# Two adaLN groups of layer 1 moved beside its modulation, and local attention scores in two passes with stacked parts

## The chip, the cores and the metric

The kernel runs on one core of a Trainium2 chip. A core has TensorE (PE in the profile), VectorE (DVE), ScalarE (ACT), GpSimd (POOL), and SyncE (SP), whose queue issues most of the loads. The metric is the device time of one execution in microseconds; smaller is better.

## The reference

Two layers over 256 context and 256 latent tokens of width 1024. Each modulates its input by adaLN, runs three token mixers (S5, latent attention, local attention), merges them with gates, and then runs sixteen experts of which each takes the tokens it wants. Only the latent stream is returned, so layer 1 updates no context.

```
def adaln_params(cond, lp):
    return jnp.split(jax.nn.silu(cond) @ lp['w_ada'] + lp['b_ada'], 6, axis=-1)
...
def trunk_layer(xc, xl, c, c_ctx, lp, row, col, update_ctx):
    mod_l = [m[:, None, :] for m in adaln_params(c, lp)]
    ...
    hl = modulate(xl, mod_l[0], mod_l[1])
    yc, yl = token_mixer(hc, hl, lp, row, col, update_ctx)
    xl = layer_norm(ALPHA * xl + mod_l[2] * yl, lp['ln1_g'], lp['ln1_b'])
    fl = expert_choice_ffn(modulate(xl, mod_l[3], mod_l[4]), lp)
    xl = layer_norm(ALPHA * xl + mod_l[5] * fl, lp['ln2_g'], lp['ln2_b'])
...
def window_branch(qc, kc, vc, ql, kl, vl, sink, row, col, update_ctx):
    ...
    qb = axial_rope(q, row, col)...          # latent queries, rotated
    s_band = jnp.einsum('bnqkgd,bnskd->bnkgqs', qb, kb) * WIN_SCALE      # banded, rotated keys
    s_ctx = jnp.einsum('bnqkgd,bskd->bnkgqs', qpb, kc) * WIN_SCALE       # plain queries, context keys
    p = jax.nn.softmax(jnp.concatenate([s_band, s_ctx, sk], axis=-1), axis=-1)
```

The six modulation vectors form three groups of two (group 0: the mixer's shift and scale; 1: its gate and the experts' shift; 2: the experts' scale and gate). A layer's input product and S5 need group 0 only.

## The kernel before

An fp32 product whose operands are activations and weights is made of f32r parts: `split` and `put` (L428 to L436) write a high part by ScalarE and the difference by VectorE or GpSimd, and `mm3` adds three products, high by high, high by low, low by high. All matmuls are issued from one line, L247, transposes from L250, loads from L233, so a row is told from another by its tile: `sc`, `mm`, `F`, `ad` and `tp` are PSUM tags, `big` holds the queries and keys of the attentions, `extra` and `wc` the parts of branch outputs and weights, `arena` everything else in fp32.

**adaLN groups.** `ada_group(l, g)` (L377) loads sixteen pieces of `w_ada`, 512 KB each, through a ring of staging buffers, and multiplies each by four fp32 matmuls of 32 columns, side by side in four column groups, into the bank `ad`: 64 matmuls a group, which the profile records twice each. Then come one addition, four transposes and the copies into `modT`. In layer 0 the groups (layer 0; 1), (0; 2), (1; 0), (1; 1), (1; 2) stand in the queue `adaq`. `step()` (L211) runs one piece of filler from `fillq` (gates, branch products) and then as much of `adaq` as the filler's cost times `ADA` allows. The mixers call `tick()` to let filler in between their own rows; the order of each engine is then set by a scheduler from dependencies and its own estimates. Layer 1's groups 1 and 2 end up between the gated unit of S5 (about 264 us) and the end of layer 0's local attention (402 us).

**Layer 1's front.** `modulated_split` (L492) finishes the layer norm of each row block, transposes it (two `tp` banks of four), and writes high and low parts of the modulated rows by ScalarE (L521) and VectorE (L522). `step` of `s5_product` multiplies them by the first columns of `w_in`, four chunks of 128x2x512, into four banks (`mm`, `mm`, `F`, `ad`).

**Local attention.** `win_proj` builds per pair of heads the plain queries QP, the rotated queries QR and the keys KW, each with its high and low part as separate columns, head a on rows 64a to 64a+63. The rotation multiplies by a 128x128 permutation, two f32r passes for queries and one fp32 matmul for keys, and adds cosine and sine products (L1249 to L1251). `win_branch` scores a tile of head a and 128 queries by `mm3` on the head's 64 rows, against 256 context and 256 latent keys: six passes of 256 columns, then a mask of 128 by an identity product. Layer 0 has sixteen such latent tiles and eight context tiles (six passes, no mask), layer 1 sixteen latent tiles. Softmax follows (maximum L1062, exponential L1069, normalisation L1075), then transposes and the product with the values.

Of the kernel before, what the change touches and what calls it, by code (L numbers as in the profile page):

```python
# [45 lines left out]
def _constants():  # L46
# [27 lines left out]

    _ROUND.append(np.concatenate([pm, np.where(k <= q, 0.0, big)], 1).astype(np.float32))
    parts["iota"] = np.tile(np.arange(1, 33, dtype=np.float32), (128, 1))
# [85 lines left out]
class Net:  # L162
# [329 lines left out]
    def modulated_split(self, l, x, in_place, step, stats):  # L492
# [37 lines left out]
        step(part, 3)  # L530
        next(self.first, None)
        self.unrot(htmp=3)
# [697 lines left out]
    def win_proj(self, l, h, full):  # L1230
# [4 lines left out]
        self.bg = [self.block(f"big{i}", F32R) for i in range(3 if full else 2)]  # L1235
        parts = lambda i, o, f, n: self.bg[i][:, o:o + 2 * f * n].rearrange("p (f r n) -> p f r n", f=f, r=2)
        QP, QR, KW = parts(0, 0, 4, NQ), parts(1, 0, 4, 256), parts(1, 2048, 2, 512)
        kf = self.buf("wkf", 512)

        def rope(dst, src, two=None):  # L1240
# [10 lines left out]
            nc.gpsimd.tensor_tensor(dst if two is None else t1, t1, t2, op=OP.add)  # L1251
            if two is not None:
                self.put(dst, t1)
            self.free("wr1", "wr2")
# [7 lines left out]
        v.tensor_copy(kf[:, 0:256], kp[:, 0:256])  # L1262
        rope(kf[:, 256:512], kp[:, 256:512])
        for kv in range(2):
            own, other = [slice(64 * a, 64 * a + 64) for a in (kv, 1 - kv)]
            self.put(KW[own, kv], kf[own])
            self.copy(KW[other, kv], KW[own, kv].bitcast(F32), "a" if kv else "v")
        for f in range(4):
            pt = self.ps("mm" if f % 2 == 0 else "F")
            w = self.wchunk(self.w_in(l, 1184 + f * 128, 1312 + f * 128), KT, 128)  # L1270
            for k in range(KT):
                self.mm3(pt[:, q0:], w(k), h(k, slice(q0, 512)), k == 0, k == KT - 1)
            self.put(QP[:, f], pt[:, q0:])
            rope(QR[:, f], pt[:, 256:], QP[:, f, :, 256 - q0:])
        self.free("wkf", "wkp")
        return QP, QR, KW

    def win_branch(self, l, Z, QP, QR, KW, full, tick):
# [5 lines left out]
        rows = [slice(0, 64), slice(64, 128)]  # L1284
        two = lambda t, c: (t[:, 0, c], t[:, 1, c])
        pv = lambda t: t.rearrange("p (a n) -> p a n", a=2)
        for hp in range(4):
# [3 lines left out]
            for qt in range(2):  # L1291
# [4 lines left out]
                for a in range(2):  # L1296
                    self.mm3(sc[a][:, 0:256], two(QP[rows[a], hp], qc), two(KW[rows[a], kv], slice(0, 256)), True, True)
                for a in range(2):
                    self.mm3(sc[a][:, 256:512], two(QR[rows[a], hp], qs), two(KW[rows[a], kv], slice(256, 512)),
                             True, False)  # L1300
                for a in range(2):
# [6 lines left out]
            if full:  # L1308
                sc = [self.ps("sc").rearrange("p (a n) -> p a n", a=2) for _ in range(2)]
                for qt in range(2):  # L1310
                    for a in range(2):
                        self.mm3(sc[a][:, qt], two(QP[rows[a], hp], slice(qt * 128, qt * 128 + 128)),
                                 two(KW[rows[a], kv], slice(0, 256)), True, True)
                for a in range(2):
# [412 lines left out]
    def build(self, layers=(0, 1), stop=None):  # L1727
# [3 lines left out]
        with tc.tile_pool(name="main", bufs=1) as main, \  # L1731
# [10 lines left out]
            self.const = main.tile([128, NCONST], F32, name="const")  # L1742
            self.round = main.tile([128, 384], F32R, name="round")
            self.idnr, self.permr, self.maskr = [self.round[:, 128 * i:128 * i + 128] for i in range(3)]
            arena = main.tile([128, self.ARENA_COLS], F32, name="arena")
# [49 lines left out]
    def layer(self, l, x, nxt):  # L1795
# [5 lines left out]
        with tc.tile_pool(name=f"parts{l}", bufs=1, reuse_waits="tile") as self.R:  # L1801
# [3 lines left out]
            if full:  # L1805
                self.load(self.const[:, 128:], self.ins["const"][:, 128:])
                self.load(self.buf("round", 256), self.ins["round"])
            h = self.modulated_split(l, x, [full or t < 2 for t in range(4)], step, self.stats)
            self.free(*[f"x{t}" for t in range(4 if full else 2)])
            if full:  # L1810
                nc.scalar.activation(self.round[:, 0:128], self.c("idn"), AF.Copy)
                nc.scalar.activation(self.round[:, 128:], self.A.at("round", 256), AF.Copy)
                self.free("round")
# [134 lines left out]
    ADA = [1.0, 0.4]  # L1948

    FEED_OUT = [[0, 1] * 4, [0, 1] * 4]  # L1950
    FEED_BRANCH = [0, 1]
# [74 lines left out]
```

## Time and profile before

| | |
|---|---|
| median of the runs | 2080.92 us |
| lowest and highest | 2080.52, 2082.33 us |
| profiled execution | 2081.91 us |
| its span | 2080.1 us |
| granted TensorE clock, mean | 0.917 |
| TensorE, VectorE, ScalarE, GpSimd busy | 87%, 50%, 29%, 21% |

The profiled execution took 1.8 us more than its span. The shares are averages over stages with different limits, so stages are to be read one by one. In the span, layer 0's mixer ends near 410 us, its experts fill the time to about 1190 us, layer 1's mixer starts at 1222 us, and its experts end the program.

### The profile page before, as it was taken

How to read it: one execution, taken by the hardware profiler on the slowest of the kernel's cores; microseconds unless marked ns; L12 is line 12 of the kernel's file. 1: busy time of each engine (PE TensorE's matmuls, PEld its weight loads, DVE VectorE, ACT ScalarE, POOL GpSimd, SP SyncE). 2: the span in 40 equal slices, each digit the busy share in tenths (PEclk: the TensorE clock that was granted, in tenths of full speed). 3: DMA queues.
4: the chain of work that ended last, by engine and by line, in shares of the span. 5: the costliest groups of instructions: out<-in, count | busy, mean ns of one | idle time of the engine just before them, and what ended most of it. 6: DMA issues, size and time to landing. Idle time of an engine off the chain costs nothing.

```text
span 2080.1 us, 31699 instructions
## 1 busy us (share of the span) xinstructions
PE 1800.9 (87%) x12421; PEld 1116.5 (54%) x12421; DVE 1030.1 (50%) x2433; ACT 603.5 (29%) x1354; POOL 444.6 (21%) x590
## 2 busy tenths in 40 slices
PE   7898999999998699999799979999998876676665
PEld 5866566677776534334233358887886532232222
DVE  6867656656537712323465276977767321010102
ACT  3354343444433321000111075354553100000000
POOL 4745420011135100001334034640114000000000
PEclk9999999999999899999999989998999887686867
DMA  9256736222237689999999813541367799999996
GB/s 348 80 158 226 245 120 200 92 71 72 63 132 264 262 332 421 421 422 415 417 415 349 335 47 99 155 121 51 103 216 301 282 421 421 421 421 422 420 421 279
DMA packets 173013, 543.88 MB, mean 261 GB/s; under 512 B 18752, under 2 KB 101952, under 8 KB 122688
## 3 DMA queue, kind: packets, MB, share of 16 engines
q1 hardware_dynamic: 172864, 541.86, 68.4%
q8 instruction: 98, 1.61, 0.3%
q14 instruction: 51, 0.42, 0.1%
HBM read 540.77 MB, written 1.05 MB: 260 GB/s over the span
## 4 chain that ended last, share of the span: by engine, by line
PE 55%; DMA 25%; DVE 14%; issue 2%; ACT 2%; POOL 2%; SPq 0%; POOLq 0%; DVEq 0%; ACTq 0%
PE sc L247 17%; PE mm L247 16%; PE F L247 13%; DMA arena<-in_w_down 5%; PE ad L247 4%; PE tp L250 4%; DMA arena<-in_w_up 4%; DMA arena<-in_w_gate 3%; DVE wc L431 2%; DVE arena L572 2%; DMA big<-in_w_gate 2%; DMA h<-in_w_gate 2%; DMA arena<-in_w_in 2%; DMA arena<-in_w_ada 2%; DVE arena L885 1%
## 5 line engine op out<-in xcount | busy, mean ns | idle before, releaser
L247 PE MATMUL F<-h,wc 128*128 128x256 f32 (+1 forms) x1200 | 233.3, 345 | 2.0 <-DVE wc L431 2.0
L247 PE MATMUL sc<-arena,xs 128*32 128x256 f32 (+1 forms) x1336 | 190.4, 528 | 40.1 <-DMA arena<-in_w_up 23.3
L428 ACT ACTIVATE wc<-arena 128x512 fp32r<-128x512 f32 (+2 forms) x280 | 170.6, 619 | 180.6 <-PE F L247 63.7
L250 PE MATMUL tp<-const,arena 128*128 128x128 f32 (+2 forms) x815 | 141.7, 297 | 79.1 <-DVE arena L291 12.2
L247 PEld LDWEIGHTS F<-h,wc 128*128 128x128 f32 x1200 | 185.8, 191 | 33.2 <-issue 6.2
L247 PE MATMUL mm<-arena 128*32 128x256 f32 (+5 forms) x1244 | 186.8, 462 | 17.3 <-DMA arena<-in_w_down 10.0
L431 DVE TENSOR_TENSOR wc<-arena,wc 128x512 fp32r<-128x512 f32 (+2 forms) x205 | 158.9, 787 | 84.6 <-ACT wc L428 84.0
L431 POOL TENSOR_TENSOR wc<-arena,wc 128x512 fp32r<-128x512 f32 (+2 forms) x75 | 98.1, 1307 | 382.6 <-ACT wc L428 340.3
L1678 DVE TENSOR_TENSOR arena<-mm,arena 32x512 f32<-32x512 f32 (+1 forms) x128 | 70.9, 554 | 217.4 <-PE mm L247 215.9
L250 PEld LDWEIGHTS tp<-const,arena 128*128 128x128 f32 (+2 forms) x815 | 97.8, 149 | 145.0 <-issue 35.6
L242 ACT ACTIVATE arena<-tp 128x512 f32<-128x512 f32 (+3 forms) x142 | 62.1, 463 | 346.3 <-PE tp L250 301.9
L247 PEld LDWEIGHTS sc<-arena,xs 128*32 128x32 f32 (+1 forms) x1336 | 61.1, 132 | 144.7 <-issue 76.7
L247 PEld LDWEIGHTS mm<-arena 128*32 128x32 f32 (+2 forms) x1244 | 76.8, 137 | 102.0 <-issue 51.9
L247 PE MATMUL sc<-h,xs 128*32 128x256 f32 (+1 forms) x752 | 110.8, 526 | 19.9 <-DMA h<-in_w_gate 11.2
L264 POOL TENSOR_TENSOR lnq<-lnq,k 128x1 f32<-128x1 f32 x22 | 14.4, 658 | 501.4 <-DVE lnq L311 471.1
L1655 DVE TENSOR_TENSOR arena<-arena,sc 128x512 f32<-128x512 f32 (+1 forms) x32 | 17.8, 555 | 181.3 <-PE sc L247 181.0
L247 PE MATMUL sc<-big,xs 128*32 128x256 f32 (+1 forms) x632 | 86.0, 525 | 23.8 <-DMA big<-in_w_up 12.7
L1653 ACT ACTIVATE arena<-sc 128x512 f32<-128x512 f32 (+1 forms) x32 | 15.7, 491 | 290.9 <-PE sc L247 290.9
L247 PE MATMUL mm<-wc,h 128*128 128x512 f32 (+2 forms) x288 | 81.3, 406 | 6.2 <-DVE wc L431 2.8
L247 PE MATMUL F<-extra,wc 128*128 128x256 f32 (+1 forms) x432 | 83.4, 337 | 3.1 <-DVE smst L1060 2.1
L1654 DVE SCALAR_TENSOR_TENSOR arena<-arena,sc 128x512 f32<-128x512 f32 (+1 forms) x32 | 17.7, 554 | 135.3 <-ACT arena L1653 135.2
L247 PEld LDWEIGHTS sc<-h,xs 128*32 128x32 f32 (+1 forms) x752 | 36.7, 132 | 87.2 <-issue 60.5
(366 smaller groups left out, 3165.4 us busy)
## 6 DMA issues: line engine op xcount, KB each, us to landing
arena<-in_w_up SPq DMA_DIRECT2D x65, 1024.0 KB, 16.6
arena<-in_w_down SPq DMA_DIRECT2D x61, 1024.0 KB, 19.8
arena<-in_w_gate SPq DMA_DIRECT2D x48, 1024.0 KB, 19.5
h<-in_w_gate SPq DMA_DIRECT2D x41, 1024.0 KB, 13.9
arena<-in_w_ada SPq DMA_DIRECT2D x80, 512.0 KB, 5.8
arena<-in_w_in SPq DMA_DIRECT2D x66, 512.0 KB, 3.9
big<-in_w_up SPq DMA_DIRECT2D x26, 1024.0 KB, 19.8
h<-in_w_down SPq DMA_DIRECT2D x26, 1024.0 KB, 18.5
```

The lines of the kernel that those rows point to most:

```text
L242: self.nc.scalar.activation(out, in_, AF.Copy)
L247: return self.nc.tensor.matmul(out, lhsT, rhs, start=start, stop=stop, skip_group_check=True)
L250: self.nc.tensor.transpose(out, in_, self.c("idn")[:n, :n])
L264: self.nc.gpsimd.tensor_tensor(out, in_, e.to_broadcast(list(in_.shape)), op=OP.pow)
L428: nc.scalar.activation(hi, src, AF.Copy)
L431: eng.tensor_tensor(lo, src, hi.bitcast(F32), op=OP.subtract)
L572: tt = lambda o, a, b, op: keep[0](v.tensor_tensor(o, a, b, op=op))
L885: v.tensor_tensor_scan(z, rb, z, 0.0, op0=OP.mult, op1=OP.add)
L1653: nc.scalar.activation(th, gu[0][:, :NF], AF.Tanh, scale=0.5)
L1654: v.scalar_tensor_tensor(th, th, 1.0, gu[0][:, :NF], op0=OP.add, op1=OP.mult)
L1655: v.tensor_tensor(th, th, gu[1][:, :NF], op=OP.mult)
L1678: v.tensor_tensor(YS[n][o:o + 32, c * NF:(c + 1) * NF], yp[r:r + 32, :NF], m5[r:r + 32], op=OP.mult)
```

## The change

Layer 0 no longer queues layer 1's groups 1 and 2. A generator `ada_behind` runs them in layer 1 while `modulated_split` runs: ahead of each pair of transposed units it advances by as many steps as `BEHIND` says, a step being two loads and eight matmuls. It has a ring of ten buffers and uses a bank of tag `sc`; what is left runs behind the last unit.

In the local attention the parts of a head are stacked on the rows: of head a, the rows 64a hold the high part and the other 64 rows the low part, and the keys the other way round. A score is then one pass over the head's 64 rows (high by high) and one over all 128 rows (high by low plus low by high): two passes where there were three. For this `put_heads` writes each half of the rows apart, and the rotation is made by two 64x64 fp32 matmuls.

```
@@ ada
+    def ada_behind(self, l):
+        stg = self.astg
+        self.astg = self.rot("ast", 1024, 10)
+        rows = [self.buf(f"adar{i}", 512) for i in range(2)]
+        gens = [self.ada_group(l, g, True, "sc", rows[g - 1]) for g in (1, 2)]
+        for n in self.BEHIND:
+            for _ in range(n):
+                while gens and next(gens[0], None) is None:
+                    gens.pop(0)
+            yield
+        for g in gens:
+            for _ in g:
+                pass
...
@@ modulated_split
         step(part, 3)
-        next(self.first, None)
+        for _ in self.first:
+            pass
...
@@ win_proj
+        def put_heads(dst, src):
+            for a in range(2):
+                nc.scalar.activation(dst[rows[a], a], src[rows[a]], AF.Copy)
+                v.tensor_tensor(dst[rows[1 - a], a], src[rows[a]], dst[rows[a], a].bitcast(F32), op=OP.subtract)
...
-            if two is None:
-                self.mm(pp[:, :256], self.permr.bitcast(F32), src, True, True)
-            else:
-                for r in range(2):
-                    self.mm(pp[:, :256], self.permr, two[:, r], r == 0, r == 1)
+            for r in rows:
+                self.mm(pp[r, :256], self.permr[r].bitcast(F32), src[r], True, True)
...
-            self.put(QP[:, f], pt[:, q0:])
-            rope(QR[:, f], pt[:, 256:], QP[:, f, :, 256 - q0:])
+            put_heads(QP[:, f], pt[:, q0:])
+            self.copy(kp[:, 0:256], pt[:, 256:], "a")
+            rope(QR[:, f], kp[:, 0:256])
...
@@ win_branch
+        def score(out, q, k, a, qc, kc, stop):
+            self.mm(out, q[rows[a], a, qc], k[rows[a], 1 - a, kc], True, False)
+            self.mm(out, q[:, a, qc], k[:, a, kc], False, stop)
...
-                    self.mm3(sc[a][:, 0:256], two(QP[rows[a], hp], qc), two(KW[rows[a], kv], slice(0, 256)), True, True)
+                    score(sc[a][:, 0:256], QP[:, hp], KW[:, kv], a, qc, slice(0, 256), True)
...
@@ the layer
+            if not full:
+                self.first = self.ada_behind(l)
...
-                self.adaq += [self.ada_group(nxt, g) for g in range(3)]
+                self.adaq += [self.ada_group(nxt, 0)]
...
+    BEHIND = (0, 0, 2, 3, 3, 3, 3, 2)
```

Three places show how the rows move. First TensorE in the second half of layer 0's local attention: `sc` are the scores, `tp` the transposes of probabilities, `mm` their products with the values, `F` the branch products that serve as filler, `ad` group 2 of layer 1. Before:

```order
L247 MATMUL ad_3233<-arena,silu_c 32x256 x8
L250 MATMUL tp_3375<-const,arena 128x128
L247 MATMUL mm_3324<-arena 64x256
L247 MATMUL sc_3326<-big_2418,big_2417 128x256 x6
L250 MATMUL tp_3381<-const,arena 128x128
L250 MATMUL tp_3375<-const,arena 128x128 x3
L250 MATMUL tp_3381<-const,arena 128x128 x3
L247 MATMUL sc_3412<-big_2418,big_2417 128x256 x3
L247 MATMUL sc_3412<-big_2418 128x256 x3
L247 MATMUL sc_3412<-round 128x128
L247 MATMUL ad_3233<-arena,silu_c 32x256 x12
```

The change, where the second half begins:

```order
L247 MATMUL F_3350<-extra_2632,wc 128x512
L247 MATMUL sc_3082<-big_2396,big_2395 128x256 x2
L247 MATMUL sc_3082<-big_2396 128x256 x2
L247 MATMUL sc_3082<-round 128x128
L250 MATMUL tp_3045<-const,arena 128x128 x4
L247 MATMUL mm_2998<-arena 64x256
L247 MATMUL sc_3083<-big_2396,big_2395 128x256 x2
L247 MATMUL sc_3083<-big_2396 128x256
L250 MATMUL tp_3051<-const,arena 128x128 x4
L247 MATMUL sc_3083<-big_2396 128x256
L247 MATMUL sc_3083<-round 128x128
L247 MATMUL mm_2998<-arena 64x256 x4
```

The adaLN rows are gone, and the last row of filler now stands ahead of the first score of the second half; none stands behind it until the attention ends.

Second, TensorE at the front of layer 1: `tp` are the transposes of the modulation, `mm`, `F` and `ad` with `wc` the four banks of the S5 input product. Before:

```order
L250 MATMUL tp_8487<-const,arena 128x128 x3
L250 MATMUL tp_8497<-const,arena 128x128 x3
L250 MATMUL tp_8507<-const,arena 128x128 x4
L250 MATMUL tp_8517<-const,arena 128x128 x4
L250 MATMUL tp_8527<-const,arena 128x128 x4
L247 MATMUL mm_8481<-wc,h_8485 128x512 x2
L247 MATMUL mm_8482<-wc,h_8485 128x512 x2
L247 MATMUL F_8483<-wc,h_8485 128x512 x2
L247 MATMUL ad_8484<-wc,h_8485 128x512 x2
```

The change, with `sc_8300` the bank of group 1:

```order
L250 MATMUL tp_8279<-const,arena 128x128 x3
L250 MATMUL tp_8289<-const,arena 128x128 x3
L247 MATMUL sc_8300<-arena,silu_c 32x256 x16
L250 MATMUL tp_8321<-const,arena 128x128 x4
L247 MATMUL sc_8300<-arena,silu_c 32x256 x20
L250 MATMUL tp_8361<-const,arena 128x128 x4
L247 MATMUL sc_8300<-arena,silu_c 32x256 x8
L250 MATMUL tp_8401<-const,arena 128x128 x4
L247 MATMUL sc_8300<-arena,silu_c 32x256 x8
L247 MATMUL mm_8273<-wc,h_8277 128x512
L247 MATMUL mm_8274<-wc,h_8277 128x512
L247 MATMUL F_8275<-wc,h_8277 128x512
```

Fifty-two matmuls of group 1 (thirteen loads) now stand ahead of the first row of the product; the other seventy-six of groups 1 and 2 (nineteen loads) stand in sixteen pieces between the product's rows that follow.

Third, SP's queue, behind the last loads of layer 0's experts (`in_w_down`). Before:

```order
L233 DMA h_5760<-in_w_down 128x2048 x2
L233 DMA h_5761<-in_w_down 128x2048 x2
L233 DMA arena<-in_w_in 128x2x512 x2
L233 DMA arena<-in_w_in 128x2x288
L233 DMA arena<-in_w_in 128x2x128
L233 DMA arena<-in_w_in 128x2x288
L233 DMA arena<-in_w_in 128x2x128
L233 DMA arena<-in_w_in 128x2x288
L233 DMA arena<-in_w_in 128x2x128
```

The change:

```order
L233 DMA h_5552<-in_w_down 128x2048 x2
L233 DMA h_5553<-in_w_down 128x2048 x2
L233 DMA arena<-in_w_ada 128x1024 x6
L233 DMA arena<-in_b_rep 128x512
L233 DMA arena<-in_w_ada 128x1024 x7
L233 DMA arena<-in_w_in 128x2x512
L233 DMA arena<-in_w_ada 128x1024 x10
L233 DMA arena<-in_w_in 128x2x512
L233 DMA arena<-in_w_ada 128x1024
L233 DMA arena<-in_w_in 128x2x288
L233 DMA arena<-in_w_in 128x2x128
L233 DMA arena<-in_w_ada 128x1024 x2
```

The four chunks of `w_in` for the product stood directly behind the experts' weights; now the first stands behind thirteen loads of `w_ada` and the second behind twenty-three.

## Rows read from the trace of the kernel before

**Rows 1.** The page's busy line: us, share of the span, instructions.

```profile
PE 1800.9 (87%) x12421; PEld 1116.5 (54%) x12421; DVE 1030.1 (50%) x2433; ACT 603.5 (29%) x1354; POOL 444.6 (21%) x590
```

**Rows 2.** Windows of layer 0's mixer: length, engines' busy us (instructions), clock, DMA share, GB/s.

```profile
264.80:310.00 45.20, 45.20 (x216) 27.84 (x215) 26.26 (x57) 21.71 (x47) 13.46 (x16) 1.00 0.37 116
310.00:357.90 47.90, 47.66 (x309) 31.56 (x308) 32.30 (x101) 16.61 (x51) 2.40 (x2) 1.00 0.61 195
357.90:402.40 44.50, 43.32 (x293) 27.87 (x292) 31.14 (x105) 18.21 (x56) 2.58 (x2) 0.95 0.44 141
```

**Rows 3.** Waits of TensorE from 264 to 402 us: total, times, longest.

```profile
PE tp L250 <- DVE arena L1075: 1.2, 1, 1.2
```

**Rows 4.** Windows of the expert stage and of layer 1, columns as above.

```profile
740.00:1190.00 450.00, 424.69 (x2086) 161.34 (x2084) 162.28 (x485) 57.30 (x148) 72.57 (x199) 0.99 0.99 404
1190.00:1202.00 12.00, 10.68 (x28) 4.15 (x24) 9.77 (x22) 4.57 (x12) 2.82 (x5) 1.00 0.00 1
1202.00:1222.20 20.20, 6.14 (x22) 3.61 (x20) 18.52 (x44) 15.27 (x31) 8.54 (x11) 0.62 0.09 27
1222.20:1249.00 26.80, 26.72 (x109) 25.77 (x110) 15.02 (x24) 21.07 (x38) 6.51 (x8) 0.90 0.29 83
1249.00:1284.00 35.00, 35.00 (x250) 31.88 (x250) 17.29 (x29) 22.21 (x46) 12.09 (x15) 1.00 0.33 91
1284.00:1386.00 102.00, 93.51 (x969) 85.09 (x966) 86.60 (x167) 41.30 (x114) 56.98 (x75) 0.97 0.47 135
1386.00:1401.50 15.50, 14.20 (x110) 13.37 (x108) 15.13 (x36) 11.67 (x22) 7.25 (x6) 1.00 0.35 109
1401.50:1428.60 27.10, 27.04 (x194) 23.15 (x195) 23.52 (x78) 13.25 (x36) 5.44 (x5) 1.00 0.31 95
1428.60:1457.50 28.90, 25.24 (x121) 17.22 (x119) 17.51 (x63) 10.71 (x33) 0.00 (x0) 0.70 0.06 18
```

**Rows 5.** Timeline of TensorE between the layers: start, us, what, idle before.

```profile
1219.96 1.08 PE L250 MATMUL tp<-const,arena 128*128 128x128 f32 x4 [2.64 <-DVE arena L522]
```

**Rows 6.** Windows of layer 0's mixer, tile ad alone.

```profile
264.80:357.90 93.10, 16.24 (x168) 5.26 (x168) 0.68 (x1) 0.00 (x0) 1.00 0.49 157
357.90:402.40 44.50, 6.60 (x88) 2.37 (x88) 0.69 (x1) 0.00 (x0) 0.95 0.44 141
```

**Rows 7.** Window of the second half of layer 0's attention, tile F alone.

```profile
357.90:402.40 44.50, 6.81 (x24) 4.28 (x24) 1.38 (x2) 0.00 (x0) 0.95 0.44 141
```

**Rows 8.** Timeline of TensorE in layer 1's local attention.

```profile
1421.08 1.63 PE L247 MATMUL F<-extra,wc 128*128 128x256 f32 x12
...
1428.31 0.45 PE L247 MATMUL F<-extra,wc 128*128 128x256 f32 x2
...
1434.26 0.62 PE L247 MATMUL sc<-big,big 64*128 64x256 f32 x3
...
1435.42 0.62 PE L247 MATMUL sc<-big,big 64*128 64x256 f32 x3
...
1438.73 0.77 PE L247 MATMUL sc<-big,big 64*128 64x256 f32 x3 [1.84 <-ACT arena L1069]
```

**Rows 9.** Timeline of TensorE in layer 0, with adaLN products of group 2.

```profile
384.70 1.50 PE L247 MATMUL ad<-arena,silu_c 128*32 128x256 f32 x24
386.13 1.08 PE L247 MATMUL mm<-arena 128*64 128x256 f32 x8
...
388.89 0.64 PE L247 MATMUL ad<-arena,silu_c 128*32 128x256 f32 x8
389.46 0.62 PE L247 MATMUL sc<-big,big 64*128 64x256 f32 x3
```

**Rows 10.** Timeline of VectorE where layer 1's local parts are built.

```profile
1394.21 1.40 DVE L436 TENSOR_TENSOR big<-arena,big 64x512 fp32r<-64x512 f32 x2
1395.64 0.42 DVE L436 TENSOR_TENSOR big<-F,big 128x256 fp32r<-128x256 f32 x1
```

**Rows 11.** Timeline of ScalarE in the same stretch.

```profile
1394.29 0.39 ACT L435 ACTIVATE big<-F 128x256 fp32r<-128x256 f32 x1
```

More of the change, by code (lines that the diff above doesn't have):

```diff
@@ L73, in _constants @@
     big = np.float32(-1e30 / WIN_SCALE)
-    _ROUND.append(np.concatenate([pm, np.where(k <= q, 0.0, big)], 1).astype(np.float32))
+    _ROUND.append(np.concatenate([pm[:, 0:64] + pm[:, 64:128], np.where(k <= q, 0.0, big)], 1).astype(np.float32))
     parts["iota"] = np.tile(np.arange(1, 33, dtype=np.float32), (128, 1))
@@ L1237, in win_proj, with rope @@
         QP, QR, KW = parts(0, 0, 4, NQ), parts(1, 0, 4, 256), parts(1, 2048, 2, 512)
+        rows = [slice(0, 64), slice(64, 128)]
+        def put_heads(dst, src):
+            for a in range(2):
+                nc.scalar.activation(dst[rows[a], a], src[rows[a]], AF.Copy)
+                v.tensor_tensor(dst[rows[1 - a], a], src[rows[a]], dst[rows[a], a].bitcast(F32), op=OP.subtract)
         kf = self.buf("wkf", 512)
-        def rope(dst, src, two=None):
+        def rope(dst, src, two=True):
             pp = self.ps("sc")
-            if two is None:
-                self.mm(pp[:, :256], self.permr.bitcast(F32), src, True, True)
-            else:
-                for r in range(2):
-                    self.mm(pp[:, :256], self.permr, two[:, r], r == 0, r == 1)
+            for r in rows:
+                self.mm(pp[r, :256], self.permr[r].bitcast(F32), src[r], True, True)
             t1 = self.buf("wr1", 256)
@@ L1250, in rope @@
             v.tensor_tensor(t2, pp[:, :256], self.c("wsin"), op=OP.mult)
-            nc.gpsimd.tensor_tensor(dst if two is None else t1, t1, t2, op=OP.add)
-            if two is not None:
-                self.put(dst, t1)
+            nc.gpsimd.tensor_tensor(t1 if two else dst, t1, t2, op=OP.add)
+            if two:
+                put_heads(dst, t1)
             self.free("wr1", "wr2")
@@ L1262, in win_proj @@
         v.tensor_copy(kf[:, 0:256], kp[:, 0:256])
-        rope(kf[:, 256:512], kp[:, 256:512])
+        rope(kf[:, 256:512], kp[:, 256:512], False)
         for kv in range(2):
             own, other = [slice(64 * a, 64 * a + 64) for a in (kv, 1 - kv)]
-            self.put(KW[own, kv], kf[own])
-            self.copy(KW[other, kv], KW[own, kv].bitcast(F32), "a" if kv else "v")
+            hi, lo = KW[own, kv, 1 - kv], KW[own, kv, kv]
+            nc.scalar.activation(hi, kf[own], AF.Copy)
+            v.tensor_tensor(lo, kf[own], hi.bitcast(F32), op=OP.subtract)
+            self.copy(KW[other, kv], KW[own, kv, ::-1].bitcast(F32), "a" if kv else "v")
         for f in range(4):
@@ L1296, in win_branch @@
                 for a in range(2):
-                    self.mm3(sc[a][:, 0:256], two(QP[rows[a], hp], qc), two(KW[rows[a], kv], slice(0, 256)), True, True)
+                    score(sc[a][:, 0:256], QP[:, hp], KW[:, kv], a, qc, slice(0, 256), True)
                 for a in range(2):
-                    self.mm3(sc[a][:, 256:512], two(QR[rows[a], hp], qs), two(KW[rows[a], kv], slice(256, 512)),
-                             True, False)
+                    score(sc[a][:, 256:512], QR[:, hp], KW[:, kv], a, qs, slice(256, 512), False)
                 for a in range(2):
@@ L1311, in win_branch @@
                     for a in range(2):
-                        self.mm3(sc[a][:, qt], two(QP[rows[a], hp], slice(qt * 128, qt * 128 + 128)),
-                                 two(KW[rows[a], kv], slice(0, 256)), True, True)
+                        score(sc[a][:, qt], QP[:, hp], KW[:, kv], a, slice(qt * 128, qt * 128 + 128), slice(0, 256), True)
                 for a in range(2):
@@ L1742, in build @@
             self.const = main.tile([128, NCONST], F32, name="const")
-            self.round = main.tile([128, 384], F32R, name="round")
-            self.idnr, self.permr, self.maskr = [self.round[:, 128 * i:128 * i + 128] for i in range(3)]
+            self.round = main.tile([128, 320], F32R, name="round")
+            self.idnr, self.permr, self.maskr = self.round[:, 0:128], self.round[:, 128:192], self.round[:, 192:320]
             arena = main.tile([128, self.ARENA_COLS], F32, name="arena")
@@ L1806, in layer @@
                 self.load(self.const[:, 128:], self.ins["const"][:, 128:])
-                self.load(self.buf("round", 256), self.ins["round"])
+                self.load(self.buf("round", 192), self.ins["round"])
+            if not full:
+                self.first = self.ada_behind(l)
             h = self.modulated_split(l, x, [full or t < 2 for t in range(4)], step, self.stats)
@@ L1811, in layer @@
                 nc.scalar.activation(self.round[:, 0:128], self.c("idn"), AF.Copy)
[L1812 removed]
+                nc.scalar.activation(self.round[:, 128:], self.A.at("round", 192), AF.Copy)
                 self.free("round")
```

10 lines of the change are left out of this document (6 added, 4 removed).

## The prediction

> **What bounds the kernel now.** First the busy line of the page: TensorE is at work 87% of the span and no other engine above 50% [rows 1], so it is TensorE's stretches that count, but not alike. I read them by windows. Layer 0's mixer, from the gated unit to the end of the local attention, is TensorE's: 45.20 of 45.20, 47.66 of 47.90 and 43.32 of 44.50 us busy [rows 2], and its only wait of note in 138 us is 1.2 us for a softmax result [rows 3]. The expert stages are the DMA's: 99% of its time at 404 GB/s from 740 to 1190 us [rows 4]. Their loads are let go by the mixer before them, so what the mixer loses or gains moves them as a block. Between the layers TensorE is nearly idle: from 1202 to 1222.2 it works 6.14 us at a granted clock of 0.62 while VectorE works 18.52, and its transposes wait for VectorE's modulated rows (L522) [rows 4, 5]. Then layer 1's input product and what follows keep it at 26.72 of 26.80 and 35.00 of 35.00; the S5 stage has VectorE at 86.60 of 102 beside TensorE's 93.51; the building of the local queries and keys has VectorE at 15.13 of 15.50; the first half of the local attention is TensorE's (27.04 of 27.10), and its second half, where no filler is left, takes 28.90 us at a clock of 0.70 [rows 4].
>
> **Groups 1 and 2 leave layer 0.** Their 256 matmul records take 16.24 us before 357.9 and 6.60 behind it [rows 6]; 357.9 is where the second half of the twenty-four local tiles (sixteen latent, eight context) begins. The eight transposes go from one place to the other and are left out at both.
>
> The first half is full, so its terms add: 93.1 us, less 16.2, plus what the order moves in. All the branch filler that stood in the second half (24 matmuls, 6.8 us [rows 7]) now stands ahead of it: +6.8. Dearer scores, twelve tiles at 0.15 (below): +1.8. Five rotations, each by two fp32 matmuls of a quarter of the array in place of two f32r passes or one fp32 matmul: a 256-column record costs (1.63 - 0.45)/10 = 0.118 us [rows 8]; two fp32 matmuls are four records, 0.47, and entering and leaving their shape 0.39, against 0.24 now, +0.62. If both quarters run at once it is +0.39. Five of them cost 2.0 to 3.1; I take 2.7. Sum: 88.2, a gain of 4.9.
>
> The second half has 44.5 - 6.6 - 6.8 = 31.1 us of its own work, 32.9 with the scores: that is its lower bound. For the upper bound the nearest row is layer 1's second half, which has no filler either: eight latent tiles in 28.9 us, with waits of 1.84 us such as the one for an exponential (L1069), and half speed [rows 4, 8]. By tiles this is 43.4 for twelve. Context tiles are independent work, so I take the middle, 38.5: a gain of 6.0. What is late there is each tile's exponential and normalisation, with the next transposes behind it on TensorE. Layer 0: -10.9, from -6.0 to -16.5.
>
> **The scores in two passes.** Now a latent tile has six 64-row passes of 256 columns and a mask of 128: 1434.26 to 1435.42, 1.16 us [rows 8]. The columns alone are 6 x 0.118 + 0.06 = 0.77, so the two changes of shape (into the 64 rows, and back for the mask) cost 0.39, 0.195 each. Behind the change each tile runs 64, 128, 64, 128 and the mask: four passes, 0.53 with the mask, and four changes, 0.78: 1.31, or +0.15. The Trainium skill, page "TensorEngine Tiling (Array Packing)", section "Key Properties", says that changing the tiling mode, not just the tile, drains TensorE. By that rule alternating modes costs what I charge; counted by columns alone the same tile would be 0.24 us cheaper than now, as the page's section "The Problem" (an array underused where the contraction is 64 or less) would have it. No row has a 64- and a 128-row pass alternating within one tile, so the price is bounded: -0.24 without changes, +0.15 with.
>
> **Groups 1 and 2 come to layer 1's front.** 128 matmuls, that is 32 loads of 512 KB with four matmuls (eight records) each. From 24 records in 1.43 us to the next start and 8 in 0.57 [rows 9], a record is 0.054, a load's share 0.43, and what is left, 0.14, is a change on one side: 0.29 for an insertion with both. The order puts 13 loads' work in four pieces ahead of the product's first row: 6.7 us at full speed, 13.4 at half, in an idle of 20.2 - 6.1 = 14.1. I cost it at nothing; the cover is the modulation on VectorE. Queued behind each piece are the transposes of the next row block, for which the modulation's copies wait; the longest piece, 20 matmuls, is 2.4 us against the 2.64 that a transpose waits there now [rows 5]. Without that cover it is +6.7.
>
> The other 19 loads' work stands in sixteen pieces behind the product's start, where TensorE has no idle time: 19 x 0.43 + 16 x 0.29 = 12.8. Against it, the product now starts at half speed (0.90 over 26.8 us, so 2.7 us lost [rows 4]); an engine busy before it may save 1 of these. I take +12, from 9 (no piece costs a change, some half speed saved) to 18 (the early work ends late by 5). VectorE's S5 stage starts from this product, and all of it shifts.
>
> The loads: 32 x 0.52 MB at 404 GB/s are 42 us, and 1190 to 1249 is 59 us with a DMA share of 0.00 to 0.29 [rows 4]. On SP's queue the product's first weights now stand behind 13 of them and the third behind 23, with a ring of ten, so the 23rd is let go only by TensorE's 13th piece of work. Two of four weight loads cover half the product, 13 us; I cost it at nothing.
>
> **Building the parts.** In layer 1 this stretch is VectorE's. Eight pairs of copy and difference on 128 rows become sixteen on 64 rows. A difference of 128x256 takes 0.42, two of 64x512 take 1.40 [rows 10]: columns set the price, rows do not. So VectorE gets 8 x 0.41 = 3.3 us more and ScalarE 8 x 0.39 and four copies, 4.7, into 3.8 idle [rows 4, 11]. I take +3.5, from 1 to 4.5 (in layer 0 it lies beside a full TensorE, and only the rotation is charged). Scores in layer 1: eight tiles in the full half +1.2, eight in the unfilled one +0.8: +2, from 0 to 2.4. Layer 1's local branch: +5.5.
>
> **Sum.** -10.9 + 12 + 5.5 = +6.6. The profiled execution took 2081.9, of which 2080.1 was span; the median of the runs is 1.0 lower, 2080.9. So 2080.9 + 6.6 = 2087.5; I say 2087.
>
> **The rivals.** A, the other side: changes of shape cost nothing once both passes write one bank, so each tile falls by 0.24 instead of rising by 0.15. On the forty latent and context tiles this is 15.6 us against the sum where all of them are on the path (2072), and 7.8 if only the full halves count (2079.5). It decides from 10.3 us, a tile of 1.05. For it: four passes in place of six. Against it: the 0.39 us measured around every tile. B: layer 0's second half, though without filler, runs at its own work, 32.9 us: -5.6, 2081.5, no change. For it: VectorE is busy 31.14 of 44.5 there, so its chain alone would fit [rows 2]; against it, layer 1's second half. C: the product waits for its third weights, or for the ring: half the idle bandwidth goes to loads that are not needed yet. The 23rd load would be issued at the product's start and the weights land some 23 us behind the second pair's use at worst, 13 of it covered: +10, 2097. For it: one queue in order; against it, an idle DMA from 1190 on. D: the move comes without a price in layer 1, since the sixteen pieces slip into gaps that the modelled ends of matmuls cover up: half of the 12.8, 2081. For it: the product's window has ScalarE, which splits its weights, at 21.07 of 26.80; against it, TensorE's 26.72 there [rows 4].
>
> **How the numbers follow.** A measurement here can tell 0.2%, 4.2 us, from no change: faster is below 2076.7, slower above 2085.1. My forecast has 0.50 (slower 0.38, same 0.10, faster 0.02: its terms' ranges together give 2080 to 2096), A 0.17 (faster 0.12, same 0.05), B 0.13 (faster 0.06, same 0.05, slower 0.02), C 0.13 (slower), D 0.07 (faster 0.04, same 0.03). Faster 0.24, same 0.23, slower 0.53. The range, 2073 to 2098, leaves out the far end of A and what goes beyond C.
>
> **What would show it.** In the profile behind the change: layer 0 from 264.8 to the output product shorter by 6 to 16 us, its second half at 37 to 41 us with a clock below 0.9; a latent tile at 1.3 us from its first pass to the next tile; between the layers TensorE at work 12 us or more before the product, and from the product's start to the S5 stage 10 to 14 us more than the 62 of now; the local parts 3 us longer. The prediction is wrong if a tile takes 1.05 us or less, if the second half stays full, or if TensorE waits for weights in the product.

## The result and the profile after

The changed kernel takes 2109.99 us (median of 4 runs, 2109.72 to 2111.27) against 2080.72 before in the same runs. The medians give a ratio of 1.0141; the ratio on record is 1.0134, interval 1.0122 to 1.0146. It is 29 us slower; the forecast was 6 us slower, with 2098 as its upper end.

The busy line of the page, after, beside [rows 1]: TensorE is busy 13.5 us longer, though with 60 instructions fewer, and no other engine more than 10.

```profile
PE 1814.4 (86%) x12361; PEld 1116.3 (53%) x12361; DVE 1034.6 (49%) x2449; ACT 613.5 (29%) x1378; POOL 441.4 (21%) x590
```

Windows of layer 0's mixer, after, the same three as in [rows 2]. The first and the last are no longer full (40.87 of 45.20, 39.71 of 44.50), and the last runs at a clock of 0.82: the work that left has been replaced in part by waiting and by a slower clock.

```profile
264.80:310.00 45.20, 40.87 (x158) 26.15 (x158) 31.84 (x65) 27.12 (x60) 14.48 (x17) 0.98 0.23 70
310.00:357.90 47.90, 47.77 (x206) 32.67 (x205) 30.82 (x107) 17.88 (x57) 1.93 (x2) 0.95 0.12 34
357.90:402.40 44.50, 39.71 (x166) 23.93 (x167) 28.48 (x110) 17.04 (x56) 1.89 (x2) 0.82 0.05 13
```

Windows of layer 1, after, cut at the events of [rows 4]: from the last expert work to the product, from the product to S5, S5, and the building of the local parts up to the first score. They were 20.2, 61.8, 102 and 15.5 us and are 3.1, 14.8, 2.6 and 9.3 longer.

```profile
1200.65:1223.90 23.25, 12.30 (x127) 5.92 (x125) 17.95 (x45) 14.13 (x29) 8.38 (x10) 0.83 0.66 234
1223.90:1300.50 76.60, 75.79 (x499) 60.65 (x501) 33.22 (x57) 46.18 (x86) 17.06 (x21) 0.96 0.54 185
1300.50:1405.10 104.60, 95.48 (x988) 87.17 (x986) 89.65 (x170) 40.88 (x114) 57.88 (x77) 0.95 0.47 132
1405.10:1429.90 24.80, 16.96 (x120) 13.96 (x118) 21.33 (x46) 16.22 (x34) 7.22 (x7) 0.93 0.27 86
```

TensorE at the front: first the product's start before, then the rows after. Three pieces (a piece is a run of adaLN matmuls between other rows) wait for their own loads, 2.4 us together, and the product's first row then waits 1.44 for ScalarE's split of its weights.

```profile
1222.28 2.10 PE L247 MATMUL mm<-wc,h 128*128 128x512 f32 x4 [1.23 <-ACT h L521]
```

```profile
1217.99 1.07 PE L247 MATMUL sc<-arena,silu_c 128*32 128x256 f32 x16 [0.88 <-DMA arena<-in_w_ada]
...
1220.52 0.64 PE L247 MATMUL sc<-arena,silu_c 128*32 128x256 f32 x8 [0.88 <-DMA arena<-in_w_ada]
1221.82 0.64 PE L247 MATMUL sc<-arena,silu_c 128*32 128x256 f32 x8 [0.66 <-DMA arena<-in_w_ada]
1223.89 1.24 PE L247 MATMUL mm<-wc,h 128*128 128x512 f32 x2 [1.44 <-ACT wc L446]
...
1246.81 0.87 PE L247 MATMUL ad<-wc,h 128*128 128x512 f32 x3
1247.52 1.58 PE L247 MATMUL mm<-wc,h 128*128 128x512 f32 x6
1248.93 0.39 PE L247 MATMUL F<-wc,h 128*128 128x512 f32 x1
...
1255.12 0.86 PE L247 MATMUL ad<-wc,h 128*128 128x512 f32 x3
1255.91 0.64 PE L247 MATMUL sc<-arena,silu_c 128*32 128x256 f32 x8
1256.48 1.80 PE L247 MATMUL mm<-wc,h 128*128 128x512 f32 x6
1258.21 0.64 PE L247 MATMUL sc<-arena,silu_c 128*32 128x256 f32 x8
```

ScalarE's split had itself waited 2.75 us, for the load of these weights:

```profile
1223.21 2.19 ACT L446 ACTIVATE wc<-arena 128x512 fp32r<-128x512 f32 x4 [2.75 <-DMA arena<-in_w_in]
```

A piece also slows its neighbours. A three-matmul row of the product takes 0.71 to the next start (1246.81 to 1247.52), and 0.79 ahead of a piece (1255.12 to 1255.91). A six-matmul row takes 1.41 (1247.52 to 1248.93), and 1.73 between two pieces (1256.48 to 1258.21): 0.08 of the 0.32 more belongs to the piece behind it, as for the row of three, and 0.24 to the piece ahead of it. With the piece's own 0.57 (1255.91 to 1256.48) that is 0.08 + 0.57 + 0.24 = 0.89 for one load.

TensorE where layer 1's parts are built, after: two waits, 5.17 and 2.68 us, for ScalarE's copy that feeds the rotation, and half speed behind the first (22 filler matmuls in 3.90 us; ahead of the waits 24 took 3.14).

```profile
1420.64 1.12 PE L247 MATMUL sc<-arena,round 64*64 64x256 f32 x4 [5.17 <-ACT arena L242]
1421.69 3.90 PE L247 MATMUL F<-h,wc 128*128 128x256 f32 x22
...
1429.28 0.65 PE L247 MATMUL sc<-arena,round 64*64 64x256 f32 x4 [2.68 <-ACT arena L242]
1429.86 0.70 PE L247 MATMUL sc<-big,big 64*128 64x256 f32 x2
```

What kept ScalarE: its second copy of a tile (L1262) waits for VectorE's first difference (L1263), which itself had stood in VectorE's queue. VectorE's row, then ScalarE's:

```profile
1410.76 0.42 DVE L1263 TENSOR_TENSOR big<-mm,big 64x256 fp32r<-64x256 f32 x1
```

```profile
1411.21 0.38 ACT L1262 ACTIVATE big<-mm 64x256 fp32r<-64x256 f32 x1 [1.90 <-DVE big L1263]
...
1419.33 0.85 ACT L1262 ACTIVATE big<-arena 64x256 fp32r<-64x256 f32 x2
```

The last row is the same pair of copies with its source in `arena` and not in a PSUM bank: the two run without a wait between them. That points to the shared source bank, and not to the buffer `big` that both engines write, as what the copies wait for.

### The profile page after: what moved, and what is told of

Its sections match the earlier page's. It is cut to its first block, busy times and chain, and to the rows that moved or that the text cites. A ratio compares the mean times of both kernels' runs of the same rounds, so it can differ in the third digit from the quotient of the medians.

```text
span 2109.5 us, 31614 instructions
## 1 busy us (share of the span) xinstructions
PE 1814.4 (86%) x12361; PEld 1116.3 (53%) x12361; DVE 1034.6 (49%) x2449; ACT 613.5 (29%) x1378; POOL 441.4 (21%) x590
## 4 chain that ended last, share of the span: by engine, by line
PE 58%; DMA 21%; DVE 14%; ACT 2%; issue 2%; POOL 2%; SPq 0%; POOLq 0%; DVEq 0%; ACTq 0%
PE sc L247 19%; PE mm L247 17%; PE F L247 14%; PE tp L250 4%; DMA arena<-in_w_down 4%; PE ad L247 4%; DMA arena<-in_w_up 3%; DVE arena L591 2%; DMA big<-in_w_up 2%; DMA arena<-in_w_gate 2%; DMA h<-in_w_gate 2%; DMA big<-in_w_gate 2%; DMA big<-in_w_down 2%; DVE arena L904 2%; DVE wc L449 2%
## 5 line engine op out<-in xcount | busy, mean ns | idle before, releaser
L247 PEld LDWEIGHTS F<-h,wc 128*128 128x128 f32 x1200 | 188.0, 194 | 32.9 <-issue 7.3
L250 PE MATMUL tp<-const,arena 128*128 128x128 f32 (+2 forms) x815 | 139.0, 293 | 75.8 <-DVE arena L291 12.1
L247 PE MATMUL sc<-h,xs 128*32 128x256 f32 (+1 forms) x752 | 110.2, 522 | 18.9 <-DMA h<-in_w_gate 10.7
L247 PE MATMUL sc<-big,xs 128*32 128x256 f32 (+1 forms) x632 | 83.0, 502 | 22.6 <-DMA big<-in_w_up 12.5
L1681 ACT ACTIVATE arena<-sc 128x512 f32<-128x512 f32 (+1 forms) x32 | 15.7, 491 | 291.4 <-PE sc L247 284.3
## 6 DMA issues: line engine op xcount, KB each, us to landing
h<-in_w_gate SPq DMA_DIRECT2D x41, 1024.0 KB, 14.9
h<-in_w_down SPq DMA_DIRECT2D x26, 1024.0 KB, 18.9
```

Source lines behind the costliest of these rows:

```text
L247: return self.nc.tensor.matmul(out, lhsT, rhs, start=start, stop=stop, skip_group_check=True)
L250: self.nc.tensor.transpose(out, in_, self.c("idn")[:n, :n])
L1681: nc.scalar.activation(th, gu[0][:, :NF], AF.Tanh, scale=0.5)
```

## The experiments

All times are medians of whole executions; "before" ran beside each on the same chip (2081.5 to 2081.7). The table shows shifts in us: the start of one instruction that both traces have, less its start before. e3 leaves the two groups out, e5 puts the low parts on other rows than the scores need, and e7 and e8 sum a bank otherwise than the reference (below), so these four give prices only. Columns: *attention* is layer 0 behind its local attention (before 480.2), *front* the last layer norm between the layers (1206.0), *product* the copy of a product bank (1270.0), *S5* its end (1386.5), *score* layer 1's first local score (1401.6), *branch* behind its local attention (1473.2), *experts* layer 1's first expert input (1629.2).

| run | attention | front | product | S5 | score | branch | experts |
|---|---|---|---|---|---|---|---|
| the change | -3.1 | -1.4 | 16.5 | 18.6 | 28.3 | 30.6 | 29.4 |
| e1 stack only | 10.1 | 9.7 | 10.0 | 10.1 | 22.2 | 25.9 | 30.3 |
| e2 ada only | -19.1 | -17.2 | -1.3 | 2.9 | 2.9 | 2.9 | 2.9 |
| e3 no groups | -22.4 | -21.5 | -21.5 | -21.5 | -21.5 | -22.6 | -21.3 |
| e4 acts first | 3.5 | 7.7 | 25.1 | 27.4 | 31.0 | 37.3 | 38.7 |
| e5 one put | 12.5 | 13.4 | 13.3 | 13.4 | 16.1 | 20.2 | 20.1 |
| e6 kp two | 18.0 | 18.0 | 18.4 | 18.5 | 30.8 | 34.4 | 32.5 |
| e7 grouped | 0.3 | 3.0 | 3.3 | 3.5 | 15.5 | 10.8 | 10.1 |
| e8 all edits | -1.5 | 0.4 | 0.5 | 0.7 | 3.1 | -0.2 | 2.6 |
| e9 after fixed | -17.9 | -15.7 | 1.9 | 4.3 | 7.9 | 11.0 | 11.7 |
| e10 stack fixed | 0.7 | 3.9 | 3.7 | 3.8 | 7.9 | 7.7 | 10.7 |
| e11 ada half | -10.9 | -9.1 | -4.9 | 1.5 | 1.5 | 2.3 | 3.0 |
| e12 both, half | -11.7 | -11.0 | -5.7 | 1.9 | 5.5 | 5.3 | 6.6 |

A single profiled execution stands a few us off its median, that of e4 ten; the steps within a row are what to read.

**e1 and e2: one half of the change each.** e1 has the hunks of `win_proj`, `win_branch` and the permutation, e2 those of `ada_behind`.

> Only the stacked parts and the two-pass scores; the adaLN groups stay in layer 0. Theory: the trace of the change shows layer 1's building of the parts 11 us longer and its scores 2 us, and the same chain in layer 0; so about +13 us from layer 1 and 0 to +12 from layer 0, where adaLN filler can stand in the gaps: 2094 to 2106. Rival (the parts are slack and the front of layer 1 is the whole loss): +2 to +5, 2083 to 2086.

> Only groups 1 and 2 moved beside layer 1's modulation; scores in three passes. Theory A: the front costs +20 and layer 0, without the stacked parts, gives back about 10: +10, 2091. Rival B: layer 0's attention gives nothing by itself since VectorE's and ScalarE's chain sets it: +17 to +20, 2098 to 2101.

e1: 2110.34, ratio 1.0136 (1.0118 to 1.0155), above either expectation. e2: 2081.65, ratio 0.9998 (0.9988 to 1.0007), below either. So the whole loss is had with the stacked scores alone, and the move alone is worth nothing: it gives layer 0 19 us and takes 22 by the end of S5, 20 of them from the front on (e2's row). Together they don't add in layer 0: -19.1 and +10.1 would be -9, and the change has -3.1.

**e3: the two groups left out.**

```
-                self.adaq += [self.ada_group(nxt, g) for g in range(3)]
+                self.adaq += [self.ada_group(nxt, 0)]
+                self.nc.vector.memset(self.modT[1][:, 2:6], 0.5)
```

> The kernel before with layer 1's groups 1 and 2 left out wholly (a constant stands in their place), so it prices what layer 0 pays for them. Theory A: -10 us, 2071. Rival B: -1 to -4, 2077 to 2080. Full TensorE price, as the prediction counted it before the unfilled half: -21, 2060.

2060.72, ratio 0.9892 (0.9866 to 0.9918): layer 0 pays the groups' full TensorE price, 21 to 22 us. For want of filler the attention loses little: its second half stands idle 3.9 of 38.2 us. Both theories fall, and the third number stands.

**e4: ScalarE's copies first**, on the change.

```
-        def put_heads(dst, src):
+        def put_heads(dst, src, also=None):
             for a in range(2):
                 nc.scalar.activation(dst[rows[a], a], src[rows[a]], AF.Copy)
+            if also is not None:
+                self.copy(*also, "a")
+            for a in range(2):
                 v.tensor_tensor(dst[rows[1 - a], a], src[rows[a]], dst[rows[a], a].bitcast(F32), op=OP.subtract)
...
-            put_heads(QP[:, f], pt[:, q0:])
-            self.copy(kp[:, 0:256], pt[:, 256:], "a")
+            put_heads(QP[:, f], pt[:, q0:], (kp[:, 0:256], pt[:, 256:]))
```

> The change with one edit: of each query tile ScalarE's two high parts and its copy come first, and then VectorE's two differences; before, they alternated, and each read of the PSUM bank by one engine waited for the other's. Theory: the alternation is what makes building the parts 11 us longer in layer 1; without it 3 to 4: 2098 to 2103. Rival: it is the doubled number of differences on VectorE, which stays: 2107 to 2110.

2110.03, ratio 1.0147 (1.0118 to 1.0176): no gain in all, as the rival has it. But the alternation is gone (ScalarE's two copies at one stretch, the rotation's copy right behind, where the change had waits between):

```profile
1417.15 0.77 ACT L1262 ACTIVATE big<-mm 64x256 fp32r<-64x256 f32 x2 [0.20 <-PE mm L247]
1417.94 0.39 ACT L242 ACTIVATE arena<-mm 128x256 f32<-128x256 f32 x1
```

and in layer 1 the first score comes 18.7 us behind the end of the S5 output (1413.8 to 1432.6) where the change needs 24.8 and the kernel before 15.1: 3.6 more, not 9.7. So the mechanism holds up to the first score, and its 6 us are lost again behind it. From S5 to the experts e4 adds 11.3 us and the change 10.8 (table): at the first score VectorE still has six differences to do where the change has two, and from there to the branch the granted clock is 0.82 where the change has 0.88. In layer 0 TensorE's wait for the copy falls from 4.3 to 2.4 us, but a new wait of 1.4, for a difference that VectorE now does late, takes its place:

```profile
299.47 6.45 PE L247 MATMUL F<-h,wc 128*128 128x512 f32 x20 [1.42 <-DVE big L1266]
```

The profiled execution took 2120.2, where the three others took 2108.5 to 2110.1; it has half speed in layer 0:

```profile
380.00:400.00 20.00, 20.00 (x58) 10.30 (x56) 7.20 (x30) 4.93 (x13) 0.00 (x0) 0.50 0.00 1
```

**e5 and e6: the doubled instructions or the buffer**, on e1.

```
e5
-            for a in range(2):
-                nc.scalar.activation(dst[rows[a], a], src[rows[a]], AF.Copy)
-                v.tensor_tensor(dst[rows[1 - a], a], src[rows[a]], dst[rows[a], a].bitcast(F32), op=OP.subtract)
+            self.put(dst, src)
e6
-            self.copy(kp[:, 0:256], pt[:, 256:], "a")
-            rope(QR[:, f], kp[:, 0:256])
+            self.copy(kp[:, 256 * (f % 2):256 * (f % 2) + 256], pt[:, 256:], "a")
+            rope(QR[:, f], kp[:, 256 * (f % 2):256 * (f % 2) + 256])
```

> The stacked scores alone (as in e1_stack_only), but the parts written by one copy and one difference on 128 rows instead of two of each on 64; the low parts then lie on the wrong rows, so the scores differ, and the time tells the price of the doubled instructions. Theory: they cost about 6 us in layer 0 and 10 in layer 1 of the 29: 2094. Rival (the extra copy kp and the fp32 rotation behind it are the chain): 2105 to 2110.

> As e1_stack_only, but the copy that feeds the rotation alternates between two halves of its buffer, so the next copy needs not wait for the rotation before it. If the single buffer makes the chain: 2098 to 2104. If not, 2108 to 2112.

e5: 2101.96, ratio 1.0100 (1.0085 to 1.0115), midway. From S5 to the first score it adds 2.7 us to before where e1 adds 12.1: the doubled instructions and their alternation are nearly all of it in layer 1, and by e4 it is the alternation. In layer 0 nothing was gained, against the expectation; there e1, which has the adaLN filler, shows no wait of TensorE for ScalarE's copy that could have been saved. e6: 2115.08, ratio 1.0169 (1.0152 to 1.0186), and 12.2 in the same stretch: the buffer is not what waits. Why layer 0 is 8 us worse in e6 was not followed up.

**e7 and e8: passes grouped by shape.** e7 is made on e1; e8 adds e4's and e6's edits. `high` is the first pass of `score`, `rest` its second, and the context tiles are grouped alike. In both, each first pass of a bank's two regions starts the sum anew, so the sums in a bank are not the reference's; from e9 on only the bank's first pass does.

```
                 for a in range(2):
-                    score(sc[a][:, 0:256], QP[:, hp], KW[:, kv], a, qc, slice(0, 256), True)
+                    high(sc[a][:, 0:256], QP[:, hp], KW[:, kv], a, qc, slice(0, 256))
+                    high(sc[a][:, 256:512], QR[:, hp], KW[:, kv], a, qs, slice(256, 512))
                 for a in range(2):
-                    score(sc[a][:, 256:512], QR[:, hp], KW[:, kv], a, qs, slice(256, 512), False)
+                    rest(sc[a][:, 0:256], QP[:, hp], KW[:, kv], a, qc, slice(0, 256), True)
+                    rest(sc[a][:, 256:512], QR[:, hp], KW[:, kv], a, qs, slice(256, 512), False)
```

> As e1_stack_only, but of each tile both 64-row passes come first and then both 128-row passes, so it has two changes of shape instead of four. Theory (a change costs 0.19 us): a latent tile falls from 1.32 to about 0.94 us, forty tiles by 15 us at most, of which the full halves keep 8: 2098 to 2103. Rival (the order of shapes costs nothing, the loss is elsewhere): 2108 to 2111.

> The stacked scores alone with all three edits: ScalarE's copies first, two halves for the rotation's copy, passes grouped by shape; adaLN groups stay in layer 0. If both causes (the alternating parts, 6 to 12 us; the four changes of shape, 8 to 15) are right: 2085 to 2096, near the kernel before. If the extra differences on VectorE are the bound: 2098 to 2104.

e7: 2089.71, ratio 1.0038 (1.0023 to 1.0053): 20.6 us back, more than expected. The table has 9.8 of them in layer 0 and 8.4 between score and branch (+3.7 in e1, -4.7 in e7). A tile of e7, two 64-row passes, two 128-row passes and the mask, with the start of the tile ahead of it:

```profile
1426.92 0.38 PE L247 MATMUL sc<-big,big 64*128 64x256 f32 x1
...
1427.84 0.38 PE L247 MATMUL sc<-big,big 64*128 64x256 f32 x1
1428.06 0.28 PE L247 MATMUL sc<-big 64*128 64x256 f32 x1
1428.27 0.39 PE L247 MATMUL sc<-big,big 128*128 128x256 f32 x1
1428.49 0.28 PE L247 MATMUL sc<-big 128*128 128x256 f32 x1
1428.61 0.22 PE L247 MATMUL sc<-round 128*128 128x128 f32 x1
1428.67 1.51 PE L247 MATMUL F<-extra,wc 128*128 128x256 f32 x11
```

It takes 0.83 from its first pass to the filler behind, and the tile ahead 0.92 to this one, where the change takes 1.22 to filler (342.86 to 344.08) and 1.32 to another tile (315.10 to 316.42, both below). e8: 2085.12, ratio 1.0014 (1.0005 to 1.0024), nearly the kernel before.

**e9 to e12: both halves mended, and half the move.** e9 is the change, e10 the stacked scores alone, each with grouping and copies first; e11 is the kernel before with group 2 alone moved; e12 is e9 with group 2 alone.

```
e11 and e12, against the change
-        gens = [self.ada_group(l, g, True, "sc", rows[g - 1]) for g in (1, 2)]
+        gens = [self.ada_group(l, g, True, "sc", rows[g - 1]) for g in (2,)]
...
-                self.adaq += [self.ada_group(nxt, 0)]
+                self.adaq += [self.ada_group(nxt, 0), self.ada_group(nxt, 1)]
...
-    BEHIND = (0, 0, 2, 3, 3, 3, 3, 2)
+    BEHIND = (0, 0, 2, 3, 3, 0, 0, 0)
```

> The change with two edits: passes grouped by shape (as in e7, with the start flag of a bank's first pass alone) and ScalarE's copies ahead of VectorE's differences. Theory: the two groups' move is worth nothing by itself (e2), so this lands where e8 did: 2080 to 2090. Rival (the move pays or costs more once layer 0's attention is short of TensorE work): 2068 to 2076, or 2094 and more.

> The same two edits, adaLN groups left in layer 0, the rotation's copy in one buffer. Theory (grouping is what counts, the second half of the buffer gave nothing): 2080 to 2087. If the two-half buffer mattered in e8: 2088 to 2092.

> The kernel before with group 2 alone moved beside layer 1's modulation, so that 13 of its 16 loads' work stands in TensorE's idle time ahead of the product and 3 behind its start. Theory: layer 0 gives back half of its 19 to 22 us, 9 to 11; the front pays 3 x 0.96 us and a product that starts about 3 us late: -3 to -6 us, 2075 to 2079. Rival (the front's price is the late start and the loads on the queue, not the pieces): 0 to +5, 2082 to 2087.

> Group 2 alone moved, scores grouped by shape, ScalarE's copies first. If gains add (e10 and e11): e10's time less 3 to 6, 2075 to 2083. If the attention of layer 0 now lacks work to fill its waits: no better than e10.

e9: 2094.10, ratio 1.0053 (1.0035 to 1.0072), above its first theory and at the lower edge of the rival. e10: 2087.40, ratio 1.0025 (1.0014 to 1.0036), just above its upper edge. e11: 2082.87, ratio 1.0003 (0.9993 to 1.0013), the rival's time, though not by its reason alone. e12: 2088.66, ratio 1.0033 (1.0021 to 1.0044), no better than e10. No run but e3, which leaves work out, beats the kernel before. With the parts and the scores mended the move still costs: e9 takes 6.7 us more than e10, with intervals that just touch.

e9 shows that the two edits bring back layer 0's gain (-17.9 at attention, where the change has -3.1 and the move alone -19.1). e11 had 9.1 us left at the front and gives 10.6 back, though only three pieces stand behind the product's start. Its product starts 1.7 us late against the shift (1214.90, where 1222.28 - 9.08 = 1213.20), the pieces cost 2.5 more, and 6.4 are lost inside S5. There VectorE's order differs from the one before: its scans (L904, before L885) wait eight times for GpSimd, 5.9 us in all, where the kernel before has four such waits and two others for GpSimd, 3.6 us together, in the same stretch (1280 to 1345 us). e11, then before:

```profile
DVE arena L904 <- POOL arena L896: 5.9, 8, 0.8
```

```profile
DVE arena L885 <- POOL arena L877: 2.1, 4, 0.9
DVE arena L875 <- POOL arena L901: 1.5, 2, 0.8
```

These 2.3 us more are a part of the 6.4 at most.

## Why the prediction was wrong

The sign, the mechanism of the scores and the half speed were right; two terms were too small and one gain too large. By stages, predicted against measured: layer 0 -10.9 and -1.4 (up to the front), the front +12 and +20.0, layer 1's local branch +5.5 and +10.8 (up to the experts); the sums are +6.6 and +29.4. What failed: the parts were said to fit into the idle time of engines, the loads at the front to cost nothing, and an insertion was priced too low. Term by term:

**Scores.** Predicted 1.31 us for a tile, measured 1.32 (315.10 to 316.42, below), and 0.92 grouped (1426.92 to 1427.84 in e7). That a change of shape costs 0.19 us was right, and e7, which takes two away, gives 0.40 a tile: 16 us if all forty tiles are on the path, of its 20.6. Rival A is out. The Trainium skill, page "TensorEngine Tiling (Array Packing)", section "Key Properties", says that changing the mode drains TensorE; the tiles of the change and of e7 agree, with four changes against two.

**Building the parts.** The step that failed: "VectorE gets 8 x 0.41 = 3.3 us more and ScalarE 8 x 0.39 and four copies, 4.7, into 3.8 idle", hence +3.5. It measured +9.7 to the first score. What I had not priced is the order of the instructions: four reads of one bank, ScalarE, VectorE, ScalarE, VectorE, then a fifth by ScalarE that feeds the rotation, each waiting for the one ahead. e4 and e5 show it, and e6 excludes the rotation's buffer. That e4, without the alternation, has +3.6 is no proof of my 3.5: e5, which has neither the doubled instructions nor the alternation, still has +2.7.

In layer 0 I charged only the rotation, since the rest "lies beside a full TensorE". That cover was the adaLN filler, which the same change takes away: in e1, with the filler, TensorE has no wait for ScalarE's copy there, and in the change it waits 4.3 us in all. From the gated unit of S5 to the first score of layer 0, e2 (without stacked parts), then the change:

```profile
265.90:302.53 36.63, 36.63 (x142) 25.34 (x140) 22.59 (x52) 20.02 (x44) 12.33 (x16) 1.00 0.24 76
```

```profile
264.85:308.08 43.23, 38.90 (x153) 24.90 (x152) 31.22 (x64) 26.62 (x58) 13.76 (x16) 1.00 0.22 68
```

TensorE is busy 2.3 us longer, close to the 2.7 that I charged for the rotations, and the other 4.3 is the waiting. TensorE's rows there, after, with three tiles, the start of the second half and the output product's first row:

```profile
307.40 0.75 PE L247 MATMUL sc<-arena,round 64*64 64x256 f32 x4 [3.17 <-ACT arena L242]
308.08 1.09 PE L247 MATMUL sc<-big,big 64*128 64x256 f32 x2
...
310.09 5.08 PE L247 MATMUL F<-extra,wc 128*128 128x512 f32 x12
315.10 0.70 PE L247 MATMUL sc<-big,big 64*128 64x256 f32 x2
...
316.42 0.70 PE L247 MATMUL sc<-big,big 64*128 64x256 f32 x2
...
317.80 3.03 PE L247 MATMUL F<-extra,wc 128*128 128x512 f32 x12
...
342.86 0.69 PE L247 MATMUL sc<-big,big 64*128 64x256 f32 x2
...
344.08 1.37 PE L247 MATMUL F<-extra,wc 128*128 128x512 f32 x5
...
357.76 0.70 PE L247 MATMUL sc<-big,big 64*128 64x256 f32 x2
...
399.26 2.93 PE L247 MATMUL mm<-wc,big 128*128 128x512 f32 x6
```

Behind the wait of 3.17 us the granted clock is 0.53:

```profile
308.08:315.10 7.02, 7.02 (x19) 5.03 (x17) 3.39 (x11) 1.70 (x5) 0.73 (x1) 0.53 0.10 34
```

The tile there takes 2.01 us to its filler (308.08 to 310.09), later 1.22, and the twelve filler matmuls 5.08, later 3.03: half speed cost 2.8 us more. The first half of the attention ended at 357.8 where it had been predicted to gain 4.9 us; it gained 0.1. The second half took 41.5 (357.76 to 399.26), not 38.5.

**Layer 0 without the filler.** Rival B's outcome, the full price back, came true for the move alone, but not by its mechanism. e2 reaches the output product 18.9 us earlier than the kernel before. The row before, then e2's, with the start of its second half:

```profile
402.43 2.73 PE L247 MATMUL mm<-wc,big 128*128 128x512 f32 x6
```

```profile
344.21 0.62 PE L247 MATMUL sc<-big,big 64*128 64x256 f32 x3
...
345.88 3.03 PE L247 MATMUL F<-extra,wc 128*128 128x512 f32 x12
...
383.56 2.93 PE L247 MATMUL mm<-wc,big 128*128 128x512 f32 x6
```

The second half takes 39.4 us in e2 and 38.2 in e3, close to the 38.5 that I took (the middle of its two bounds is 38.2) and not rival B's 32.9. What was too small is the first half's gain: 13.7 in e2, where my terms without the scores and rotations give 9.4. I had moved all 24 filler matmuls out of the second half, and in e2 twelve of them still stand there (345.88, 3.0 us). In the change all 24 did move, and the waits and the half speed of the parts ate the gain.

**The front.** Predicted +12 (9 to 18), measured +20.0 in the change and 20.1 in e2. The product started 3.0 us late (1223.89, where 1222.28 less the 1.4 gained ahead of it is 1220.9), against "I cost it at nothing": the loads did wait, as rival C has it and as one of the signs of being wrong, for less than a third of rival C's price. The nineteen loads' work took 14.9 and not 12.8 (from the product's start to the copy of its bank): a piece of one load costs 0.89 and not 0.72, since an insertion costs 0.46 beside the load's own 0.43 and not 0.29. By these prices the sixteen pieces would be 15.5. Rival D, half of the price, is out. And S5 took 2.1 more.

Summed, the change has -1.4 at the front, +20.0 from there to the end of S5, +9.7 to the first score, and +1.1 behind it (2.3 more up to the branch, 1.2 less from there to the experts): 29.4. Why S5 loses 2 to 8 us whenever pieces run ahead of it (2.1 in the change, 6.4 in e11, 7.6 in e12) stays open: e11 shows VectorE in another order with more waits for GpSimd, but no run put the old order back.

## What to carry to other kernels

Counting passes is not counting time: put passes of one shape next to each other, since here the order of four passes was worth more (0.40 us a tile) than dropping two of six (0.24, from 1.16 to 0.92). When one read of a bank becomes several, try letting one engine do all its reads before the other starts, and look for where the time goes then: here it gave 6 us up to the first score and nothing in the total by itself (e4). When a change takes filler away from a stage and lengthens a chain in the same stage, price the chain without its cover. And price an insertion by rows of the kind that it will stand between.

## What the runs showed of the hardware

The granted clock added to waits. Behind TensorE's wait of 3.17 us in layer 0 its rows ran at 0.53 for 7 us and took 2.8 us more, nearly as much as the wait itself. In e4's profiled execution TensorE was busy all of 380 to 400 us at 0.50, the lower of its two levels, and that execution took 2120.2 us at a mean granted clock of 0.908, where the others took 2108.5 to 2110.1 at 0.917 to 0.919.

A change between 64-row and 128-row passes cost 0.19 to 0.20 us: 1.32 us for a tile with four changes, 0.92 for the same passes with two.
